# Sample tokens with the weights as the stationary operand: q, k, v of layer 1 of 2 and v, o of layer 2 of 2

## The chip, the core and the metric

The kernel runs on one NeuronCore of a Trainium2 chip. The metric is the device time of one execution in microseconds (us), the median of several runs. Five engines work side by side, each with its own queue: TensorE (PE in the profile; its weight loads have a row of their own, PEld), VectorE (DVE), ScalarE (ACT), GpSimd (POOL) and SyncE (SP), which here only issues DMAs.

A matmul on TensorE has two sides. `PE.matmul(out, l, r)` loads `l` into the array first (LDWEIGHTS, the stationary side) and then streams the columns of `r` through it (MATMUL, the moving side). The result has one partition per column of `l` and one column per column of `r`. The profile writes such a matmul as `128*16 128x512`: 128 rows by 16 stationary columns, then 128 rows by 512 moving columns.

## The reference

One inference step of a two-layer decoder trunk, for a prompt of 1024 tokens and eight sample tokens (one each of eight sequences with states of their own), 1032 tokens in all, model width 1024. Both layers normalise, project, mix and add the result to the residual:

```
u = hn @ w_in
# layer 0 (even): q | k | v | gate | z | xBC | dt
#   q, k: 8 heads of 64, partly rotated; dilated window attention, and a Mamba-2 scan
# layer 1 (odd):  q | k | v | o | i | f | z
#   mLSTM matrix memory, 8 heads of 256: h = sigmoid(o) * num / den, then head norm and silu(z)
```

The prompt goes through chunked forms of attention, scan and memory; each sample token takes one step against its cached keys and values or its state. All tensors are float32. What matters here are the products of the eight sample tokens' normalised activations with q, k, v (and dt) of layer 0, and with v and o of layer 1.

## The kernel before

Activations are kept transposed, feature on the partition: eight tiles `xh[k]` of 128 features by 1032 tokens. The matmuls take operands of type float32r. The kernel splits each float32 operand into a high part, its cast to float32r, and the remainder (`split`, L89: a ScalarE cast, then a subtraction on VectorE or GpSimd), `xh` and `xl` for activations, `wh`/`wl` and the like for weights, and `mm3` (L103) adds three products for each k: high by high, high by low, low by high.

**Layer 0, q, k, v (L517 to L574).** The loop runs over four groups `g` (two attention heads each, 128 columns each of q, k and v and four of dt: W1 = 388) and nine token blocks `b`. For b = 0 to 7 a block is 128 prompt tokens, for b = 8 the eight sample tokens. `qkv_block` takes the activations as the stationary side (128 or 8 columns) and 388 weight columns as the moving side: 24 matmuls into a PSUM tile `pq` from the pool of three banks (`MM`, L71). ScalarE copies q and k out, VectorE dt and v, GpSimd applies the rotation. For b = 8 the rows are stored at once to `qd`, `kd`, `vd` for the sample attention. The group's weights lie in four buffers of a ring of five (`w1p`, L308); `w1_fetch` splits the next group's as buffers come free. `qk_T` (L550) transposes q and k of the block before. `att_pump` (L511) takes steps of the prompt attention of earlier groups from a queue and puts them between; a `side` function runs in the middle of a block's matmuls.

The normalised activations come from `xn0_piece` (L324), in pieces of 256, 256 and 520 tokens; its `sink` (L223) scales and splits them. `sink` already knows a target `xs`, which nothing in layer 0 uses.

**Layer 1, v and o (L1464 to L1489).** For each of eight heads the weights `wv` are 1024 by 512 (256 columns of v, 256 of o). `vo_block` goes over nine blocks c. For c = 0 to 7 it is 24 matmuls of 128 stationary token columns by 512 weight columns. For c = 8 the stationary side is `xsm[:, k]`, 16 columns: the high parts of the eight sample tokens and then their low parts. Sixteen matmuls (8 k, high and low weights) give 16 rows of 512 in one PSUM tile, and ScalarE copies them out. Rows 0 to 7 and rows 8 to 15 go to the DRAM tile `svo` by four stores, and `dml_group` (L1367), which updates the samples' memory states for two heads at a time, loads both halves and adds them.

After each `vo_block(c)` comes `mstage(hd, c)` (L1491): `ml_prep(c)`, `ml_main(c - 1)` and `ml_out(c - 2)`, the chunked memory of the prompt. `ml_prep` makes the scores `mS`, `ml_main` the matmuls `mN` and `mC`, the state `Cst` and its split `mCh`, `mCl` for the next chunk, and the head norm `md`, `mx`; `ml_out` transposes `mx` into `mH`. Their PSUM tiles come from the pool of five banks (`X`, L74). So behind the sample block stand `ml_main(7)` and `ml_out(6)`, and the next head's projection `pf`.

A scheduler orders each engine's queue when the kernel is built: roughly the order of the program, but an instruction whose inputs it reckons ready can go ahead of one that would have to wait. The order is fixed before the kernel runs.

Of the kernel before, what the change touches and what calls it, by code (L numbers as in the profile page):

```python
# [7 lines left out]
F32R = mybir.dt.float32r  # L8
# [20 lines left out]
def body(ctx, tc, I, O):  # L29
# [35 lines left out]
    def SM(name, shape, bufs=2, dt=F32):  # L65
        return cur["sm"].tile(shape, dt, tag=name, name=name, bufs=bufs)
# [4 lines left out]
    def MM(name="mm"):  # L71
        return ps.tile([128, 512], F32, tag="mm", name=name, bufs=PS_MM)
# [10 lines left out]
    def C(name, shape, src=None, p=None):  # L83
        t = (p or cur["cst"]).tile(shape, F32, name=name)
        if src is not None:
            load(t, src)
        return t

    def split(hi, lo, src, eng=V):  # L89
        A.copy(hi, src)  # L90
        eng.tensor_tensor(lo, src, hi.bitcast(F32), sub)  # L91
# [80 lines left out]
    normw = C("normw", [128, 2, 8], I["normw"], gcst)  # L172
    ones = C("ones", [128, 128], None, gcst)
    G.memset(ones, 1.0)
    mhalf = C("mhalf", [128, 16], None, gcst)
    G.memset(mhalf, -0.5)

# [45 lines left out]
    def sink(src, wcol, pbs, hi, lo, eng=V, xs=None):  # L223
        scaled(src, src, wcol, pbs)
        split(hi, lo, src, eng)
        if xs is not None:
            split(xs[:, 0:8], xs[:, 8:16], src[:, 512:520])

    def pairs(tiles):
        return lambda k, c0, w: tiles[k // 2][:, (k % 2) * 520 + c0 : (k % 2) * 520 + c0 + w]  # L230
# [93 lines left out]
    def xn0_piece(i, c0, n):  # L324
        cs = slice(c0, c0 + n)
        box = {}

        def square(k):
            x = xs0[i](k)
            if i == 0:  # L330
                if k == 0:
                    t = S("acc")
                    box["acc"] = [t[:, :n], t[:, 512 : 512 + n]]
                hsum(box["acc"][k % 2], x, k < 2, k % 2 == 1)
                return
            if k == 0:
                box["acc"] = [TMP("acc")[:, :n]]
            hsum(box["acc"][0], x, k == 0)

        def stat():  # L340
            box["r"] = stat_r(box["acc"], n, 1.0 / 1024, 1.0)

        def bcast():
            box["p"] = r_bcast(box["r"], n)

        def out(k):
            sink(xs0[i](k), normw[:, 0, k : k + 1], box["p"], xh[k][:, cs], xl[k][:, cs], (V, G)[k % 2])

        return [lambda k=k: square(k) for k in range(8)], [stat, bcast], [lambda k=k: out(k) for k in range(8)]

# [160 lines left out]
    def att_pump(n, limit):  # L511
        for _ in range(n):
            if attq and attq[0][0] < limit:
                attq.popleft()[1]()


    def qkv_block(g, b, wp, side):  # L517
        m = 128 if b < 8 else 8
        c0 = b * 128
        p = MM("pq")  # L520
        terms = []
        for k in range(8):
            wv = slice((k % 2) * W1, (k % 2) * W1 + W1)
            terms.append((xh[k][:, c0 : c0 + m], xl[k][:, c0 : c0 + m], wp[k // 2][0][:, wv], wp[k // 2][1][:, wv]))
        mm3(p[:m, :W1], terms, side)
        qk = SM("qk", [128, 4, 64], 3)
        A.copy(qk[:m].rearrange("p a b -> p (a b)"), p[:m, 0:256])
        V.tensor_copy(dtr[:m, b, 4 * g : 4 * g + 4], p[:m, 384:388])
        ra = SM("ra", [128, 4, 16])
        cb = rot_c[:m, b : b + 1, :].broadcast_to([m, 4, 16])  # L530
        s1 = rot_s[:m, b : b + 1, 0:8].broadcast_to([m, 4, 8])
        s2 = rot_s[:m, b : b + 1, 8:16].broadcast_to([m, 4, 8])
        G.tensor_tensor(ra[:m, :, 0:8], qk[:m, :, 8:16], s1, mult)
        G.tensor_tensor(ra[:m, :, 8:16], qk[:m, :, 0:8], s2, mult)
        G.tensor_tensor(qk[:m, :, 0:16], qk[:m, :, 0:16], cb, mult)
        G.tensor_tensor(qk[:m, :, 0:16], qk[:m, :, 0:16], ra[:m], add)
        if b < 8:
            V.tensor_copy(vt[g][:, c0 : c0 + 128], p[:, 256:384])
            store(O["ak"][c0 : c0 + 128, g * 128 : g * 128 + 128], qk[:, 2:4, :].rearrange("p a b -> p (a b)"))
            return qk  # L540
        gs = slice(g * 128, g * 128 + 128)
        vs = SM("vs", [8, 128])
        A.copy(vs, p[:8, 256:384])
        store(O["aks"][:, gs], qk[:8, 2:4, :].rearrange("p a b -> p (a b)"))
        store(O["avs"][:, gs], vs)
        store(qd[:, gs], qk[:8, 0:2, :].rearrange("p a b -> p (a b)"))
        store(kd[:, gs], qk[:8, 2:4, :].rearrange("p a b -> p (a b)"))
        store(vd[:, gs], vs)

    def qk_T(g, b, qk):  # L550
# [4 lines left out]
        A.activation(qT[g][:, c0 : c0 + 128], pt[:, 0:128], AF.Copy, scale=-0.125)  # L555
        V.tensor_copy(kT[g][:, c0 : c0 + 128], pt[:, 128:256])

    for g in range(4):
        while len(w1r) < 4:
            w1r.append(w1_fetch(*w1q.popleft()))  # L560
        wp = [w1r.popleft() for _ in range(4)]
        qT[g], kT[g], vt[g] = S("qT"), S("kT"), S("vt")
        prev = None
        for b in range(9):
            qk = qkv_block(g, b, wp, [lambda: att_pump(2, g)] * 1)
            if prev is not None:
                qk_T(g, b - 1, prev)
            prev = qk
            if b == 7 and w1q:
                w1r.append(w1_fetch(*w1q.popleft()))  # L570
            att_pump(2, g)
            if g == 0 and b < 4:
                bpump((10, 16, 10, 0)[b])
        att_load(g)  # L574
    w1stack.close()
    wstack0 = ctx.enter_context(ExitStack())
    cur["w"] = pool("wp0", 2, wstack0)
# [467 lines left out]

        return f

    xsm = gcst.tile([128, 8, 16], F32R, name="xsm")
    hacc = st
    xh1, xl1 = [], []  # L1050

# [204 lines left out]

    hTd = D("hTd", [16, 128, NP])
    sqk = D("sqk", [2, 4, 8, 2, 256])
    svo = D("svo", [2, 2, 4, 8, 2, 256])
    mxs = C("mxs", [128, 4, 8])  # L1260
    mcv = C("mcv", [128, 32, 3])
    szs = C("szs", [128, 16, 8])
# [104 lines left out]
    def dml_group(g):  # L1367
        v32 = SM("v32", [16, 264], 1)
        o32 = SM("o32", [16, 256], 1)
        v2 = TMP("v2")[:16, :512].rearrange("p (j e) -> p j e", j=2)  # L1370
        for j, t in ((0, v32), (1, o32)):
            load(t[:, 0:256], svo[0, j, g].rearrange("b h e -> (b h) e"))
            load(v2[:, j], svo[1, j, g].rearrange("b h e -> (b h) e"))
        q = SM("dq", [128, 32], 1)
        kw = SM("dkw", [128, 32], 1)
        nn = dn4[:, g]
# [4 lines left out]
        num = SM("dnum", [128, 260], 1)  # L1381

        def prep():
            for j, t in ((0, v32), (1, o32)):
                V.tensor_tensor(t[:, 0:256], t[:, 0:256], v2[:, j], add)
            G.tensor_scalar(v32[:, 256:259], dg4[:, :, g], 1.0, None, mult)
            p = X("pvb")
            PE.matmul(p[:, 0:259], blkT, v32[:, 0:259], start=True, stop=True)
            A.copy(vb[:, 0:259], p[:, 0:259])
# [72 lines left out]
            wvr.append(wsplit(None, 1024, S("wvh", F32R), S("wvl", F32R), V, wvraw.popleft()))  # L1462

    def vo_block(hd, c, wv):  # L1464
        p = MM("pvo")
        g, h2 = divmod(hd["h"], 2)
        if c < 8:
            terms = []
            for k in range(8):
                o = (k % 2) * 512  # L1470
                terms.append((xh[k][:, c * 128 : c * 128 + 128], xl[k][:, c * 128 : c * 128 + 128], wv[k // 2][0][:, o : o + 512], wv[k // 2][1][:, o : o + 512]))
            mm3(p, terms)
            vv = (R("mvh", [128, VC]), R("mvl", [128, VC]))
            for u in range(2):
                G.tensor_scalar(vv[u][:, 256:VC], two[:, u], 1.0, None, mult)
            split(vv[0][:, 0:256], vv[1][:, 0:256], p[:, 0:256])
            tho = SM("mtho", [128, 256])
            A.activation(tho, p[:, 256:512], AF.Tanh, scale=0.5)
            hd["v", c] = (vv, tho)
        else:  # L1480
            for k in range(8):
                o = (k % 2) * 512
                for u in range(2):
                    PE.matmul(p[:16], xsm[:, k], wv[k // 2][u][:, o : o + 512], start=k == 0 and u == 0, stop=k == 7 and u == 1)
            vo8 = TMP("vo8")[:, :512]
            A.copy(vo8[:16], p[:16])
            for u in range(2):
                for j in range(2):
                    store(svo[u, j, g, :, h2], vo8[u * 8 : u * 8 + 8, j * 256 : j * 256 + 256])  # L1489

    def mstage(hd, c):  # L1491
        if c < 8:
# [22 lines left out]
    for h in range(8):  # L1515
# [51 lines left out]
        wv = [wvr.popleft() for _ in range(4)]  # L1567
        hd["C"] = SM("Cst", [128, 2, VC], 1)
        for c in range(9):
            vo_block(hd, c, wv)  # L1570
            if c == 1:
                p = X("pms")
                PE.transpose(p[:32, 0:128], t.rearrange("p a b -> p (a b)"), ident)
                t2 = TMP("mst2")[:32, :128]
                V.tensor_copy(t2, p[:32, 0:128])
                for j in range(4):
                    store(sqk[j // 2, g, :, h2, (j % 2) * 128 : (j % 2) * 128 + 128], t2[j * 8 : j * 8 + 8])
            mstage(hd, c)
            if c == 2 and h2:
                pump(1)  # L1580
            if c == 7 and h:
                dml_load(*((g, 0) if h2 else (g - 1, 3)))
# [281 lines left out]
```

## Time and profile before

| what | us |
| --- | --- |
| median of 3 runs | 2126.53 |
| lowest and highest | 2125.18, 2133.5 |
| the profiled execution | 2130.37 |
| its span, first instruction to last | 2128.5 |

Mean granted clock of TensorE in the profiled execution: 0.997 of full speed.

The profile is of one execution. Its page gives for each engine the busy time, and a chain followed back from the last instruction. A row of a group reads: line, engine, operation, output<-inputs, shapes, xcount | busy us, mean ns of one | idle time before them and who ended it. A row of the timeline reads: start us, duration us, engine, line, operation, output<-inputs, shapes, count. Durations of matmuls overlap, because they are pipelined; what one costs in a row of many is the distance from start to start. A row of the windows view reads: stretch, its length, then busy time and count for PE, PEld, DVE, ACT and POOL, then the granted clock of TensorE, the DMA engines' share and GB/s.

### The profile page before, as it was taken

To read this page: it belongs to the slowest core of one execution; us is meant where nothing else is said; L and a number is where in the kernel's file an instruction comes from. 1 tells how busy PE (TensorE), PEld (TensorE's weight loads), DVE (VectorE), ACT (ScalarE), POOL (GpSimd) and SP (SyncE) were. 2 spreads that over 40 slices of the span, in tenths; PEclk is the share of its full clock that TensorE was granted. 3 is DMA by queue.
4 is the path that set the end of the run, shared out by engine and by line. 5 is a ranking of instruction groups with operands and counts; after the bars stand their busy time and mean duration, and the time that the engine had idled before them with its cause. 6 is when DMAs were issued, how large, how long until landed. Compare 5 with 4: busy or idle time off the path is not lost.

```text
span 2128.5 us, 35218 instructions
## 1 busy us (share of the span) xinstructions
PE 2088.0 (98%) x12926; PEld 1873.7 (88%) x12926; DVE 1348.8 (63%) x3208; ACT 869.3 (41%) x1901; POOL 478.0 (22%) x1004
## 2 busy tenths in 40 slices
PE   7999999999999999999999999999999999999998
PEld 6877778998898899989899898898998988987798
DVE  7444478879987657546457565584665755756744
ACT  5434344456644334424335343253342533434321
POOL 4222100114310001241321522314214133141000
PEclk9999999999999999999999999999999999999999
DMA  5222053226575543312114133141331322416742
GB/s 162 73 74 79 14 163 105 85 75 194 185 226 167 169 162 60 90 35 85 50 64 135 41 111 98 40 145 44 99 117 37 116 78 78 140 31 213 268 163 96
DMA packets 162077, 232.30 MB, mean 109 GB/s; under 512 B 41200, under 2 KB 106976, under 8 KB 161904
## 3 DMA queue, kind: packets, MB, share of 16 engines
q1 hardware_dynamic: 161904, 230.04, 34.5%
q8 instruction: 102, 1.67, 0.3%
q14 instruction: 71, 0.58, 0.1%
HBM read 174.35 MB, written 55.62 MB: 108 GB/s over the span
## 4 chain that ended last, share of the span: by engine, by line
PE 85%; DVE 4%; DMA 2%; POOL 2%; ACT 2%; issue 1%; SPq 0%; POOLq 0%; DVEq 0%; ACTq 0%
PE pf L112 36%; PE pvo L112 16%; PE po L931 14%; PE pq L112 4%; PE mN L112 2%; PE mC L112 2%; PE pS L428 2%; PE pO L487 1%; PE mS L1294 1%; PE pT L470 1%; PE py L771 1%; POOL mCl L91 1%; PE mH L1355 1%; PE psl L777 1%; PE mS L1296 1%
## 5 line engine op out<-in xcount | busy, mean ns | idle before, releaser
L112 PE MATMUL pf<-yh,wh 128*128 128x344 f32 x1152 | 370.2, 321 | 0.0
L112 PE MATMUL pf<-yl,wh 128*128 128x344 f32 x1152 | 368.9, 320 | 0.0
L112 PE MATMUL pf<-yh,wl 128*128 128x344 f32 x1152 | 368.5, 320 | 0.0
L91 DVE TENSOR_TENSOR wl<-raw,wh 128x1024 fp32r<-128x1024 f32 x128 | 159.0, 1242 | 146.1 <-ACT wh L90 145.3
L90 ACT CAST wh<-raw 128x1024 fp32r<-128x1024 f32 x128 | 134.2, 1049 | 256.9 <-PE po L931 99.6
L112 PEld LDWEIGHTS pf<-yh,wh 128*128 128x128 f32 x1152 | 216.9, 188 | 1.3 <-ACT craw L242 1.0
L112 PEld LDWEIGHTS pf<-yl,wh 128*128 128x128 f32 x1152 | 216.5, 188 | 0.0
L112 PEld LDWEIGHTS pf<-yh,wl 128*128 128x128 f32 x1152 | 216.4, 188 | 0.0
L112 PE MATMUL pvo<-wvh,yh 128*128 128x512 f32 x512 | 206.3, 403 | 0.0
L112 PE MATMUL pvo<-wvh,yl 128*128 128x512 f32 x512 | 202.0, 394 | 0.0
L112 PE MATMUL pvo<-wvl,yh 128*128 128x512 f32 x512 | 201.5, 394 | 0.0
L112 PE MATMUL pf<-xh,wh 128*128 128x344 f32 x576 | 191.6, 333 | 0.0
L112 PE MATMUL pf<-xl,wh 128*128 128x344 f32 x576 | 186.8, 324 | 0.0
L112 PE MATMUL pf<-xh,wl 128*128 128x344 f32 x576 | 186.7, 324 | 0.0
L1282 DVE TENSOR_SCALAR mx<-mx,mbs,md 128x256 f32<-128x256 f32 x64 | 26.4, 413 | 177.7 <-POOL md L1281 177.7
L250 DVE SCALAR_TENSOR_TENSOR cout<-craw,mcw,cout 128x1024 f32<-128x1024 f32 x96 | 123.3, 1285 | 14.0 <-ACT cout L248 11.9
L931 PE MATMUL po<-oh,wl 128*128 128x512 f32 (+2 forms) x384 | 123.4, 322 | 2.8 <-DVE wl L91 2.7
L931 PE MATMUL po<-oh,wh 128*128 128x512 f32 (+2 forms) x384 | 123.6, 323 | 1.2 <-ACT oh L90 1.2
L931 PE MATMUL po<-ol,wh 128*128 128x512 f32 (+2 forms) x384 | 123.7, 323 | 0.0
L112 PEld LDWEIGHTS pvo<-wvh,yl 128*128 128x128 f32 x512 | 96.2, 188 | 22.6
L112 PEld LDWEIGHTS pvo<-wvh,yh 128*128 128x128 f32 x512 | 96.3, 188 | 20.6 <-issue 1.3
L112 PEld LDWEIGHTS pvo<-wvl,yh 128*128 128x128 f32 x512 | 96.3, 188 | 20.0
(440 smaller groups left out, 4995.7 us busy)
## 6 DMA issues: line engine op xcount, KB each, us to landing
raw<-in_wo SPq DMA_DIRECT2D x56, 512.0 KB
raw<-in_wq SPq DMA_DIRECT2D x32, 512.0 KB
raw<-in_wvo SPq DMA_DIRECT2D x32, 512.0 KB
dC<-in_mcs SPq DMA_DIRECT2D x32, 512.0 KB
out_mcs<-dC SPq DMA_DIRECT2D x32, 512.0 KB
raw<-in_wf SPq DMA_DIRECT2D x24, 512.0 KB
sE<-acd SPq DMA_DIRECT2D x16, 512.0 KB
raw<-in_wz SPq DMA_DIRECT2D x16, 512.0 KB
```

The lines of the kernel that those rows point to most:

```text
L90: A.copy(hi, src)
L91: eng.tensor_tensor(lo, src, hi.bitcast(F32), sub)
L112: PE.matmul(out, l, r, start=i == 0, stop=i == n - 1)
L250: V.scalar_tensor_tensor(o[:, :NP], raw[:, j : j + NP], w4[:, j : j + 1], o[:, :NP], mult, add)
L428: PE.matmul(p[:, :n], qT[g][hs, qs], kT[g][hs, ks], start=True, stop=True)
L470: PE.transpose(pt[:, h * n + k : h * n + k + 128], P[:, k : k + 128], ident)
L487: PE.matmul(po[h * 64 : h * 64 + 64, qs], v, PT[:, h * n + k * 128 : h * n + k * 128 + 128], start=j + k == 0, stop=j == 7 and k == nk - 1)
L771: PE.matmul(o, xd[:, h], Ev[:, h], start=True, stop=True)
L777: PE.matmul(pl, bt, xx[:, 512:1024], start=True, stop=True)
L931: PE.matmul(p[:, :m], wt[:, ws], at, start=i == 0 and q == 0, stop=i == nk - 1 and q == 2)
L1282: V.tensor_scalar(x, x, bs[:, 6:7], d[:, 2:3], sub, mult)
L1294: PE.matmul(pS[:, 0:128], hd["k"][j][:, tok], hd["q"][j][:, tok], start=j == 0, stop=j == 1)
```

## The change

Both sample projections swap their sides. A new helper `sample_cols` takes 128 weight columns at a time as the stationary side and the 16 columns `xsm[:, k]` as the moving side: for each column block m, 16 matmuls (8 k, high and low weights) into 16 columns of one PSUM tile from the pool of five. ScalarE copies the tile out, and VectorE adds the columns of the high parts to those of the low parts, which leaves the result with the weight column on the partition and the eight samples along the row. `sample_rows` turns it back: one transpose of 8 columns per block m. For layer 1 there are four blocks of 128; for layer 0 there are three of 128 and one of 4 (dt).

`xsm` is now filled in layer 0 too, in the last piece of `xn0_piece`. In layer 0 the block b = 8 returns a function that does the transposes and the rest of the old work; it runs in the middle of the next group's first block, or after the loop for the last group. In layer 0 this uses four products (high and low of both) in place of three. In layer 1 the transposes, the copy and two stores in place of four run after `mstage(hd, 8)`; `svo` loses its leading dimension, and `dml_group` two loads and two additions.

```diff
+    xsm = gcst.tile([128, 8, 16], F32R, name="xsm")
...
+    def sample_cols(n, w):
+        p = X("pxs")
+        nm = -(-n // 128)
+        ends = [min(128, n - 128 * m) for m in range(nm)]
+        for m, e in enumerate(ends):
+            for k in range(8):
+                for u in range(2):
+                    PE.matmul(p[:e, 16 * m : 16 * m + 16], w(k, u)[:, 128 * m : 128 * m + e], xsm[:, k], start=k == 0 and u == 0, stop=k == 7 and u == 1)
+        parts = TMP("parts")
+        pv = parts[:, : 16 * nm].rearrange("p (m u t) -> p m u t", m=nm, u=2)
+        sv = parts[:, 64 : 64 + 8 * nm].rearrange("p (m t) -> p m t", m=nm)
+        full = n // 128
+        for m0, m1, e in ((0, full, 128), (full, nm, ends[-1])):
+            if m1 > m0:
+                A.copy(parts[:e, 16 * m0 : 16 * m1], p[:e, 16 * m0 : 16 * m1])
+                V.tensor_tensor(sv[:e, m0:m1], pv[:e, m0:m1, 0], pv[:e, m0:m1, 1], add)
+        return sv, ends
+
+    def sample_rows(sv, ends):
+        p = X("pxr")
+        for m, e in enumerate(ends):
+            PE.transpose(p[:8, 128 * m : 128 * m + e], sv[:e, m], ident[:e, :e])
+        return p
...
-            sink(xs0[i](k), normw[:, 0, k : k + 1], box["p"], xh[k][:, cs], xl[k][:, cs], (V, G)[k % 2])
+            sink(xs0[i](k), normw[:, 0, k : k + 1], box["p"], xh[k][:, cs], xl[k][:, cs], (V, G)[k % 2], xsm[:, k] if c0 + n == T else None)
...
+        if b == 8:
+            sv = sample_cols(W1, lambda k, u: wp[k // 2][u][:, (k % 2) * W1 : (k % 2) * W1 + W1])
+            att_pump(2, g)
+            return lambda: qkv_out(g, b, sample_rows(*sv))
...
-            qk = qkv_block(g, b, wp, [lambda: att_pump(2, g)] * 1)
+            qk = qkv_block(g, b, wp, [lambda: (att_pump(2, g), late.popleft()() if late else None)] * 1)
...
+            if b == 8:
+                late.append(qk)
...
+    late.popleft()()
...
-            load(t[:, 0:256], svo[0, j, g].rearrange("b h e -> (b h) e"))
-            load(v2[:, j], svo[1, j, g].rearrange("b h e -> (b h) e"))
+            load(t[:, 0:256], svo[j, g].rearrange("b h e -> (b h) e"))
...
-            for k in range(8):
-                o = (k % 2) * 512
-                for u in range(2):
-                    PE.matmul(p[:16], xsm[:, k], wv[k // 2][u][:, o : o + 512], start=k == 0 and u == 0, stop=k == 7 and u == 1)
-            vo8 = TMP("vo8")[:, :512]
-            A.copy(vo8[:16], p[:16])
-            for u in range(2):
+            sv = sample_cols(512, lambda k, u: wv[k // 2][u][:, (k % 2) * 512 : (k % 2) * 512 + 512])
+
+            def finish():
+                vo8 = TMP("vo8")[:8, :512]
+                A.copy(vo8, sample_rows(*sv)[:8])
                 for j in range(2):
-                    store(svo[u, j, g, :, h2], vo8[u * 8 : u * 8 + 8, j * 256 : j * 256 + 256])
+                    store(svo[j, g, :, h2], vo8[:, j * 256 : j * 256 + 256])
+
+            return finish
...
-            vo_block(hd, c, wv)
+            fin8 = vo_block(hd, c, wv)
...
             mstage(hd, c)
+            if fin8:
+                fin8()
```

More of the change, by code (lines that the diff above doesn't have):

```diff
@@ L525, in qkv_block, with qkv_out @@
         mm3(p[:m, :W1], terms, side)
+        return qkv_out(g, b, p)
+    def qkv_out(g, b, p):
+        m = 128 if b < 8 else 8
+        c0 = b * 128
         qk = SM("qk", [128, 4, 64], 3)
@@ L556, in qk_T @@
         V.tensor_copy(kT[g][:, c0 : c0 + 128], pt[:, 128:256])
+    late = deque()
     for g in range(4):
@@ L1046, in operand @@
         return f
-    xsm = gcst.tile([128, 8, 16], F32R, name="xsm")
     hacc = st
@@ L1258, in body @@
     sqk = D("sqk", [2, 4, 8, 2, 256])
-    svo = D("svo", [2, 2, 4, 8, 2, 256])
+    svo = D("svo", [2, 4, 8, 2, 256])
     mxs = C("mxs", [128, 4, 8])
@@ L1369, in dml_group @@
         o32 = SM("o32", [16, 256], 1)
-        v2 = TMP("v2")[:16, :512].rearrange("p (j e) -> p j e", j=2)
         for j, t in ((0, v32), (1, o32)):
-            load(t[:, 0:256], svo[0, j, g].rearrange("b h e -> (b h) e"))
-            load(v2[:, j], svo[1, j, g].rearrange("b h e -> (b h) e"))
+            load(t[:, 0:256], svo[j, g].rearrange("b h e -> (b h) e"))
         q = SM("dq", [128, 32], 1)
@@ L1383, in prep @@
         def prep():
-            for j, t in ((0, v32), (1, o32)):
-                V.tensor_tensor(t[:, 0:256], t[:, 0:256], v2[:, j], add)
             G.tensor_scalar(v32[:, 256:259], dg4[:, :, g], 1.0, None, mult)
@@ L1464, in vo_block @@
     def vo_block(hd, c, wv):
-        p = MM("pvo")
         g, h2 = divmod(hd["h"], 2)
         if c < 8:
+            p = MM("pvo")
             terms = []
```

## The prediction

> **What bounds the kernel now.** I read the page first: the busy shares and the chain that ended last.
>
> ```profile
> span 2128.5 us, 35218 instructions
> PE 2088.0 (98%) x12926; PEld 1873.7 (88%) x12926; DVE 1348.8 (63%) x3208; ACT 869.3 (41%) x1901; POOL 478.0 (22%) x1004
> PE 85%; DVE 4%; DMA 2%; POOL 2%; ACT 2%; issue 1%; SPq 0%; POOLq 0%; DVEq 0%; ACTq 0%
> PE pf L112 36%; PE pvo L112 16%; PE po L931 14%; PE pq L112 4%; PE mN L112 2%; PE mC L112 2%; PE pS L428 2%; PE pO L487 1%; PE mS L1294 1%; PE pT L470 1%; PE py L771 1%; POOL mCl L91 1%; PE mH L1355 1%; PE psl L777 1%; PE mS L1296 1%
> ```
>
> TensorE is busy 98% and carries 85% of the chain, so a microsecond added to its stream is a microsecond of the end. Only its waits can give something back. What matters is the start-to-start spacing of its instructions, which the timeline gives (time, duration, engine, line):
>
> ```profile
> 942.26 0.40 PE L1484 MATMUL pvo<-wvl,xsm 128*16 128x512 f32 x1
> ...
> 945.53 0.39 PE L1484 MATMUL pvo<-wvl,xsm 128*16 128x512 f32 x1
> 66.29 0.34 PE L112 MATMUL pq<-w1h,xh 128*8 128x388 f32 x1
> ...
> 67.17 0.34 PE L112 MATMUL pq<-w1h,xl 128*8 128x388 f32 x1
> ```
>
> The first pair is the 2nd and the 16th sample matmul of a head: 3.27 us in 14 steps, **0.234 us** each. The second pair is five steps of a layer-0 sample block: **0.176 us** each. Both are set by the moving columns (512, 388), the short stationary load beside them hidden.
>
> **The change part by part.** The stationary side becomes 128 weight columns and the moving side 16, so the weight load is what remains. The groups of loads by form, and the two places where loads meet almost no moving columns:
>
> ```profile
> L112 PEld LDWEIGHTS pvo<-wvl,yh 128*128 128x128 f32 x512 | 96.3, 188 | 20.0
> L1296 PEld LDWEIGHTS mS<-ident,cout 128*128 128x128 f32 x128 | 16.2, 142 | 0.0
> L1484 PEld LDWEIGHTS pvo<-wvl,xsm 128*16 128x16 f32 x64 | 6.1, 95 | 7.8
> L188 PEld LDWEIGHTS pst<-ones,yacc 128*128 128x128 f32 x16 | 2.2, 191 | 0.0
> 2032.65 0.98 PEld L188 LDWEIGHTS pst<-ones,yacc 128*128 128x128 f32 x8
> L858 PE MATMUL psy<-ident,so 8*128 8x8 f32 x8 | 0.7, 204 | 0.0
> 629.29 0.66 PE L858 MATMUL psy<-ident,so 8*128 8x8 f32 x8
> ```
>
> Eight pairs of a 128-column load and a one-column matmul (pst) take 0.98 us from the first load's start to the last one's end; without that last load's 0.191 us, seven steps of **0.113 us**. The transposes psy take (0.66 - 0.204)/7 = **0.065 us**. Which one prices the new pairs? This kernel's own fp32r loads last 188 ns at 128 columns and 95 at 16, 0.83 ns a column, as the pst loads do (191); transposing loads take 142. So I take 0.113 and keep 0.065 as the low end. From above, load and matmul laid end to end bound it at about 0.12, since the 16 columns cost 16/512 of 0.234.
>
> *Layer 1, each of 8 heads.* Removed: 16 x 0.234 = 3.74 us. Added: four blocks of 16 pairs, 64 x 0.113 = 7.23 us. Added after the stage: four transposes of an 8-column stationary against the identity. Their spacing comes from two transposes with the same 128 moving columns:
>
> ```profile
> 67.35 0.38 PE L554 MATMUL pqk<-ident,qk 128*128 128x128 f32 x2
> L554 PE MATMUL pqk<-ident,qk 128*128 128x128 f32 x64 | 12.0, 274 | 0.7 <-POOL qk L536 0.7
> ```
>
> (0.38 - 0.27) = 0.11, so 0.44 us. Net +3.93 a head, **+31.4 us**.
>
> *Layer 0, each of 4 groups.* Removed: 24 x 0.176 = 4.22 us. Added: three full blocks, 48 x 0.113 = 5.42, and one of four columns, 16 pairs at 0.065 (between 0.02 and 0.113) = 1.04, and 0.39 of transposes. Net +2.63, **+10.5 us**.
>
> *Off TensorE.* The new PSUM copies, adds and the final copy lie beside other TensorE work. fin8 runs after the matmuls of mstage(hd, 8), the layer-0 transposes in the middle of the next group's first block, so those matmuls cover copy and add; uncovered they would cost about 0.5 us each time (a small cast and a subtraction take 0.19 and 0.35 in the xsm rows below). For the last group no block follows, but queued attention does. The svo stores go from four to two a head and two loads and two adds a group disappear. SP's queue gets shorter, and nothing on the path waits for it: **0**.
>
> *What is given back.* TensorE's waits, from the view of waits (total, times, longest):
>
> ```profile
> PE mH L1355 <- DVE mx L1282: 4.5, 8, 1.0
> PE mN L112 <- POOL mCl L91: 1.2, 3, 0.4
> ```
>
> The eight mH waits are one a head, right behind the sample block. A block 3.5 us longer lets the mx chain finish: **-5** (0 to -5.7).
>
> *Start.* Layer 0 now fills xsm too, eight casts and eight subtractions; the rows are those of the same work in layer 1:
>
> ```profile
> L90 ACT CAST xsm<-h x8: 193/194/197, 807.3 to 812.8; 128x8 fp32r<-128x8 f32 x8
> L91 DVE TENSOR_TENSOR xsm<-h,xsm x8: 153/352/701, 808.0 to 813.2; 128x8 fp32r<-128x8 f32 x8
> ```
>
> VectorE is the slower side of that loop: 8 x 0.15 to 0.35 = 1.2 to 2.8 us, part of it behind block b=4's matmuls: **+1** (0 to 3).
>
> *Weights of the next group.* The five-buffer ring frees a w1 buffer when its last reader ends. The old order (k outside) freed one every six matmuls; the new one (column block outside) frees all in the last, short block. The casts and subtractions queued behind:
>
> ```profile
> 65.30 1.88 POOL L91 TENSOR_TENSOR w1l<-raw,w1h 128x776 fp32r<-128x776 f32 x1 [0.35 <-ACT w1h L90]
> ...
> 66.49 0.84 ACT L90 CAST w1h<-raw 128x776 fp32r<-128x776 f32 x1 [0.20 <-PE pq L112]
> ```
>
> One buffer is ready after 0.84 + 1.88 = 2.7 us. The tail block and the next group's first two k steps (1.0 + 12 x 0.176/2) cover some 2.1: about 0.7 at each of three changes, **+2** (0 to 6). The sample block also moves from the pool of three PSUM banks to the pool of five that mS, mN, mC and mH use; its first matmul may wait for the mkl that reads the oldest: **+2** (0 to 3).
>
> Sum: 31.4 + 10.5 - 5 + 1 + 2 + 2 = **+42 us** as long as the clock holds. The profiled execution took 2130.4 (span 2128.5), the median is 2126.5; the difference moves both alike, so 2168.5.
>
> **The clock.** The windows view has the granted clock (PEclk, after the busy times):
>
> ```profile
> 338.96:342.37 3.41, 3.41 (x11) 1.66 (x9) 1.70 (x6) 0.80 (x3) 0.00 (x0) 1.00 0.02 5
> 342.37:345.78 3.41, 3.41 (x15) 2.85 (x14) 1.34 (x6) 0.00 (x0) 0.00 (x0) 0.50 0.00 0
> 1994.42:1997.83 3.41, 1.15 (x5) 0.98 (x6) 3.41 (x7) 0.17 (x1) 0.00 (x0) 1.00 0.98 321
> 1997.83:2001.25 3.42, 3.42 (x10) 2.64 (x9) 3.42 (x9) 0.46 (x1) 0.00 (x0) 0.50 0.99 361
> ```
>
> Twice the clock fell to 0.50 for one window of 3.41 us, each time after a window with few matmuls. The later one held five of 512 columns (2,560 columns), behind an idle stretch. The earlier one reads busy (by modelled ends), but held few columns:
>
> ```profile
> L428 PE MATMUL pS<-kT,qT 64*128 64x256 f32 x4 | 2.5, 724 | 0.0
> L112 PE MATMUL pf<-xh,wl 128*128 128x344 f32 x2 | 0.7, 373 | 0.0
> L112 PE MATMUL pf<-xh,wh 128*128 128x344 f32 x2 | 0.7, 346 | 0.0
> L470 PE MATMUL pT<-ident,P 128*128 128x128 f32 x2 | 0.6, 300 | 0.0
> L112 PE MATMUL pf<-xl,wh 128*128 128x344 f32 x1 | 0.3, 321 | 0.0
> ```
>
> 4 x 256 + 5 x 344 + 2 x 128 = 3,000 columns. The new blocks stream 30 pairs x 16 = **480 columns** in such a window, for 6.4 us (layer 0) or 7.2 us (layer 1). If the gate counts what streams, each block holds a whole poor window and the clock falls in all twelve; if it counts loads too, it holds. No row separates these; the column count fits both falls, so I give falling more.
>
> The Trainium skill ("TensorE: Matmul & The Clock Gate", Part 1) ties the half clock to an idle window of about 3.4 us. By that rule a block without idle time keeps its clock, which is rival A below; the trace speaks against it at 338.96, where TensorE reads busy throughout and the clock still fell, though modelled ends may hide short gaps there.
>
> Price of a fall, from rows at half clock: the first pst of the kernel, whose matmuls last 353 ns where later ones last 234, and po in the second fall's window:
>
> ```profile
> 8.47 2.14 PE L188 MATMUL pst<-ones,acc 128*128 128x1 f32 x8 [8.47 <-DVE acc L217]
> L188 PE MATMUL pst<-ones,acc 128*128 128x1 f32 x8 | 2.0, 353 | 8.6 <-DVE acc L217 8.5
> L188 PE MATMUL pst<-ones,yacc 128*128 128x1 f32 x16 | 2.2, 234 | 0.0
> 1999.72 0.63 PE L931 MATMUL po<-oh,wl 128*128 128x512 f32 x1
> ...
> 2000.57 0.63 PE L931 MATMUL po<-ol,wh 128*128 128x512 f32 x1
> ```
>
> A pair then takes (2.14 - 0.353)/7 = 0.255, a 512-column matmul 0.425. The fall comes at the end of the first whole window, 3.4 to 6.8 us into a block, 5.1 on average. In layer 1 the 2.1 us left become 4.7 (+2.6), and about 5 us of dense work behind it runs at half pace until a window has filled again, losing 45%, 2.3: **+5 a head** (3.4 to 7.3), 40 us. In layer 0 1.3 us are left, +1.6 and 2.3: **+4 a group**, 16 us. Together 42 + 56 = **+98 us, 2224.5**.
>
> **The rivals.**
> *A, the clock holds:* 2168.5. For it: loads keep the array occupied all through. Against it: 338.96.
> *B, the clock falls in each block:* 2224.5. For it: both falls.
> *C, A with a queue block.* ScalarE's copy of the new PSUM tile, and VectorE's add behind it, wait for the whole sample block. If they are queued ahead of the state's update, that chain starts only then:
>
> ```profile
> 942.01 0.87 DVE L1337 SCALAR_TENSOR_TENSOR Cst<-Cst,scl,mC 128x258 f32<-128x258 f32 x2
> ...
> 944.17 0.61 ACT L90 CAST mCh<-Cst 128x516 fp32r<-128x516 f32 x1
> ...
> 944.87 1.32 POOL L91 TENSOR_TENSOR mCl<-Cst,mCh 128x516 fp32r<-128x516 f32 x1 [1.04 <-ACT mCh L90]
> ```
>
> 2.8 us less the first mN matmuls, 2.4 a head, and about 4 in layer 0: +23 on A, 2191.5. Against it: Cst starts at 942.01 beside the block's first matmuls, with everything it needs, so a copy that waits for the block's end has no reason to stand ahead of it.
> *D, not slower:* the load is cheap, at the psy price. 704 pairs x (0.113 - 0.065) = 34 us less than A: 2134.5. Each 0.01 us of a pair is 7 us; below 0.068 the change is within 0.5%. Against it: fp32r loads of 188 ns, not 142.
>
> **How the numbers follow.** B 0.50, A 0.34, C 0.10, D 0.06. Forecast: 2224.5. B's own range is 2200 to 2240. The range goes from A's low end (short pairs at 0.02, a full give-back, no stalls: 2157) to B's upper end, 2240; it leaves out D and the tails. About 0.5% (10.6 us) can be told from no change: A, B and C are slower, 0.94; D is the same, 0.05, or with a little more, faster, 0.01.
>
> **What would show it.** Right: new pairs 0.113 apart before any fall; PEclk at 0.50 for whole 3.41 us windows after each sample block and a mean clock near 0.97 to 0.98 against 0.997; mH waits gone. A shows the same spacing and a clock of 1.00. C shows TensorE waiting for mCl or mCh once a head. D shows pairs under 0.07. Wrong altogether: TensorE's stream no longer the bound, or blocks broken up by other matmuls so that no window is poor.

## The result, and the profile after

| | before | after |
| --- | --- | --- |
| median, us | 2128.79 (5 runs) | 2214.05 (5 runs) |
| lowest and highest | 2125.18, 2133.5 | 2213.57, 2216.5 |
| ratio, 95% interval | | 1.0407 (1.0395 to 1.0419) |
| the profiled execution | 2130.37 | 2216.5 |
| its mean granted clock | 0.997 | 0.969 |

The change makes the kernel 4.1% slower, 85 us. The page of the changed kernel, the lines that answer to those of before:

```profile
span 2214.7 us, 36427 instructions
PE 2180.0 (98%) x13518; PEld 1987.2 (90%) x13518; DVE 1358.7 (61%) x3224; ACT 869.7 (39%) x1925; POOL 478.9 (22%) x1004
PE 84%; DVE 2%; ACT 1%; DMA 1%; POOL 1%; issue 1%; SPq 0%; POOLq 0%; DVEq 0%; ACTq 0%
PE pf L112 36%; PE pvo L112 16%; PE po L969 13%; PE pxs L237 4%; PE mN L112 3%; PE mC L112 2%; PE mS L1331 1%; PE pq L112 1%; PE pS L453 1%; PE pO L512 1%; PE pT L495 1%; PE py L809 1%; PE mH L1392 1%; PE mS L1333 1%; PE psl L815 0%
```

TensorE is busy 98% as before, in a span that is 86 us longer. The new pairs (pxs) hold 4% of the chain, some 89 us by that rounded share, though 704 pairs at 0.112 us would be 79 and the matmuls they replace took 47. So their price alone is not the whole loss.

The timeline shows that price (start, duration, engine, line), with the clock at 1.00 up to 68.97 us and at 0.50 behind it:

```profile
64.13 0.26 PE L237 MATMUL pxs<-xsm,w1h 128*128 128x16 f32 x1
64.24 0.26 PE L237 MATMUL pxs<-xsm,w1l 128*128 128x16 f32 x1
...
68.93 0.33 PE L237 MATMUL pxs<-xsm,w1l 128*128 128x16 f32 x1
69.11 0.36 PE L237 MATMUL pxs<-xsm,w1h 128*128 128x16 f32 x1
...
69.75 0.36 PE L237 MATMUL pxs<-xsm,w1l 128*128 128x16 f32 x1
69.97 0.17 PE L237 MATMUL pxs<-xsm,w1h 128*4 128x16 f32 x1
...
70.36 0.17 PE L237 MATMUL pxs<-xsm,w1l 128*4 128x16 f32 x1
```

From 64.13 to 68.93 are 43 steps: **0.112 us** a pair. From 69.11 to 69.75 are three steps at half clock: 0.214. The short block's 15 steps from 69.97 to 70.36, still at half clock, take 0.026 each.

The windows view around the sample block of the first head of layer 1, which begins at 964.1 (after the busy times of PE, PEld, DVE, ACT and POOL stands the granted clock):

```profile
963.26:966.67 3.41, 3.41 (x32) 3.31 (x30) 2.81 (x12) 0.91 (x2) 0.71 (x3) 1.00 0.08 19
966.67:970.08 3.41, 3.41 (x19) 3.41 (x18) 0.41 (x1) 0.00 (x0) 2.27 (x4) 0.50 0.14 38
970.08:973.50 3.42, 3.42 (x18) 3.42 (x18) 0.00 (x0) 0.00 (x0) 0.00 (x0) 0.50 0.02 5
973.50:976.91 3.41, 3.41 (x17) 3.41 (x18) 0.19 (x1) 0.21 (x1) 0.00 (x0) 0.50 0.00 0
976.91:980.33 3.42, 3.42 (x18) 3.09 (x18) 2.24 (x10) 0.05 (x1) 0.43 (x2) 0.50 0.11 38
980.33:983.74 3.41, 3.41 (x23) 3.41 (x23) 0.98 (x5) 0.52 (x1) 0.98 (x3) 1.00 0.27 82
```

The clock falls inside the block, for four whole windows, and comes back only after a window of dense work (mN, mC, the transposes). TensorE and its loads read busy all the time; what is missing is moving columns (whether that is the cause, e3 and e5 test). The same happens in each of the twelve blocks: in layer 0 stretches of 6.83, 6.83, 10.24 and 6.83 us at half clock (30.7 together), in layer 1 between 6.83 and 13.65 us a head (88.7 together). Before, two windows of 3.41 us fell, apart from the end.

The view of waits answers to that of before (total us, times, longest):

```profile
PE pO L512 <- DVE PT L500: 2.1, 5, 0.6
PE pxs L237 <- DVE mkl L1340: 1.4, 2, 0.8
...
PE pq L112 <- DVE w1l L91: 0.2, 1, 0.2
```

The 4.5 us of mH waits and the 1.2 us of mN waits are gone; the new block waits twice for its PSUM tile.

Where the 86 us lie can be read from the first pvo matmul of layer 1's first and last head. Before, then after:

```profile
878.71 0.51 PE L112 MATMUL pvo<-wvh,yh 128*128 128x512 f32 x1
...
1852.80 0.50 PE L112 MATMUL pvo<-wvh,yh 128*128 128x512 f32 x1
```

```profile
900.70 0.51 PE L112 MATMUL pvo<-wvh,yh 128*128 128x512 f32 x1
...
1930.50 0.50 PE L112 MATMUL pvo<-wvh,yh 128*128 128x512 f32 x1
```

| stretch, us | before | after | more |
| --- | --- | --- | --- |
| start to the first pvo (layer 0 among it) | 878.7 | 900.7 | 22.0 |
| one head, mean of seven | 139.16 | 147.11 | 7.95 |
| last head's pvo to the end | 275.7 | 284.2 | 8.5 |

22.0 + 7 x 7.95 + 8.5 = 86.2, the difference of the spans.

### The profile page after: what moved, and what is told of

It is laid out like the page before. It is cut to its first block, busy times and chain, and to the rows that moved or that the text cites. A ratio compares the mean times of both kernels' runs of the same rounds, so it can differ in the third digit from the quotient of the medians.

```text
span 2214.7 us, 36427 instructions
## 1 busy us (share of the span) xinstructions
PE 2180.0 (98%) x13518; PEld 1987.2 (90%) x13518; DVE 1358.7 (61%) x3224; ACT 869.7 (39%) x1925; POOL 478.9 (22%) x1004
## 4 chain that ended last, share of the span: by engine, by line
PE 84%; DVE 2%; ACT 1%; DMA 1%; POOL 1%; issue 1%; SPq 0%; POOLq 0%; DVEq 0%; ACTq 0%
PE pf L112 36%; PE pvo L112 16%; PE po L969 13%; PE pxs L237 4%; PE mN L112 3%; PE mC L112 2%; PE mS L1331 1%; PE pq L112 1%; PE pS L453 1%; PE pO L512 1%; PE pT L495 1%; PE py L809 1%; PE mH L1392 1%; PE mS L1333 1%; PE psl L815 0%
```

## The experiments

The theory: a pair of a 128-column load and 16 moving columns costs 0.112 us, more than what it replaces; and since so little streams, the clock falls in each block. The rivals: the clock answers to the loads and not to the columns; the clock costs little and the loads carry it all; the new waits do.

**One layer at a time.** e1 keeps the new form in layer 0 alone, e2 in layer 1 alone; the other layer's functions are those of before.

> Only layer 0 in the new form; layer 1 as in the kernel before. Theory (loads at 0.111 us a pair, and a clock that falls because few columns stream): per group 48 x 0.111 + 16 x 0.03 + 0.4 - 4.2 = +2.0 and about +3.7 for a fall (30.7 us at half clock over four groups, half of it lost), with +1 for the start: +24, about 2153 us (2146 to 2158); half clock behind each of the four blocks, none in layer 1 but the old one near 1998. Rival (the clock costs next to nothing, the loads carry it all): +60 or so of the 85 would have to sit in layer 1, and this run gives 2140 or less.

> Only layer 1 in the new form; layer 0 as in the kernel before. Theory: per head 64 x 0.111 + 0.4 - 3.74 = +3.8, less 0.56 of mH wait, plus 5.5 for a fall (88.7 us at half clock over eight heads, half of it lost): +8.7 a head, about 2198 us (2188 to 2203). With e1 the two parts add up to the whole change within 3 us. Rival (the parts share a cost, as a common wait): the two gains over the kernel before don't add up to 85.

e1: 2153.1 us (2148.39 to 2159.54) against 2129.31, ratio 1.0116 (1.0095 to 1.0137). e2: 2188.54, ratio 1.0281 (1.0265 to 1.0296). Both lie in their ranges, e2 at the low end. 23.8 + 59.2 = 83.0 of 85: the parts add up, and layer 1 carries most. The runs of e1 lie 11 us apart, those of the whole change 3. In e1's profile the half-clock stretches of the four groups are 6.83, 3.41, 10.24 and 6.83 us, one window fewer than in the change; the number can differ between executions. The mean clocks of e1's four runs go with their times: 0.991, 0.988, 0.988 and 0.986 for 2148.39, 2152.82, 2153.38 and 2159.54 us. Only the first has a trace, so where the others lost their clock isn't shown.

**The same loads with more columns.** e3 lets each sample matmul stream its 16 columns eight times over (`reps` is (8,)):

```diff
+                r = reps[k % len(reps)]
+                xr = xsm[:, k].unsqueeze(1).broadcast_to([128, r, 16])
                 for u in range(2):
-                    PE.matmul(p[:e, 16 * m : 16 * m + 16], w(k, u)[:, 128 * m : 128 * m + e], xsm[:, k], start=k == 0 and u == 0, stop=k == 7 and u == 1)
+                    PE.matmul(p[:e, 128 * m : 128 * m + 16 * r].rearrange("p (r t) -> p r t", r=r), w(k, u)[:, 128 * m : 128 * m + e], xr, start=k == 0 and u == 0, stop=k == 7 and u == 1)
...
```

The copy behind it, not shown here, then reads the first 16 of each 128 columns.

> Same loads, same order; each sample matmul streams 128 columns (its 16 repeated eight times) where the change streams 16, some 30 x 128 = 3,840 a window. Theory (the gate counts what streams): pair spacing stays at 0.111 us since the load sets it, the clock holds in all twelve blocks, 2155 to 2172 us at a mean clock of 0.995 or more. Rival 1 (the gate answers to the loads, or to their share of the window): falls as in the change, 2210 to 2225. Rival 2 (the clock follows something else in the new blocks, as the wait for PSUM): the same as rival 1.

2184.39 us (2178.8 to 2186.39), ratio 1.0264 (1.0247 to 1.0281): 30 us faster than the change, but slower than the 2155 to 2172 expected. In the profiled execution the mechanism is as the theory has it: the spacing stays 0.112 us (the load hides 128 columns as it hides 16), and the clock holds in all twelve blocks (two falls are left inside the run, at 214.5 and 1969.0, each behind a stall of TensorE). Two steps of e3:

```profile
69.52 0.28 PE L239 MATMUL pxs<-xsm,w1l 128*128 128x128 f32 x1
...
69.74 0.28 PE L239 MATMUL pxs<-xsm,w1l 128*128 128x128 f32 x1
```

Two windows inside a block of the same form (in e6, below), where the granted clock stays at 1.00:

```profile
964.40:967.80 3.40, 3.40 (x33) 3.40 (x32) 1.76 (x10) 0.92 (x2) 1.30 (x2) 1.00 0.17 46
967.80:971.20 3.40, 3.40 (x33) 3.40 (x32) 0.41 (x1) 0.00 (x0) 1.29 (x4) 1.00 0.02 5
```

Loads are as many and as dense as in the change, so they don't pull the clock. That execution is the fastest of the four, 2178.8 us at a mean clock of 0.995; the other three, 2184 to 2186 us, have 0.989 or 0.990, so they spent more time at half clock, and no trace shows where. What kept the time up is another thing, and it stands in the view of waits and the timeline of ScalarE in the last head:

```profile
PE pxr L253 <- DVE parts L247: 8.8, 1, 8.8
```

```profile
1973.35 1.04 ACT L90 CAST oh<-hld 128x1024 fp32r<-128x1024 f32 x1 [1.61 <-DMA hld<-hTd]
1974.30 0.20 ACT L246 COPY parts<-pxs 128x64 f32<-128x64 f32 x1
1976.87 0.57 ACT L1520 COPY vo<-pxr 8x512 f32<-8x512 f32 x1 [2.36 <-PE pxr L253]
```

The pairs of that block ended at 1964.7, but the copy of the tile stands in ScalarE's queue behind casts that wait for DMAs, and the transposes behind the copy. The queue's order is fixed when the kernel is built; why the scheduler put the copy there (it may reckon these matmuls slower than they are) isn't shown. TensorE stands idle, and the clock falls for 10.24 us. This is rival C of the prediction at another place: the change itself doesn't have it, its copy stands in front of those casts.

**Spread over the stage.** e4 leaves layer 0 as in the change. In layer 1 it computes the four column blocks at four places, with 16 columns (`sample_part`, not shown here, is `sample_cols` for a single block):

```diff
+            if c in (1, 3, 5):
+                if c == 1:
+                    svt[0] = SM("svt", [128, 4, 8], 1)
+                sample_part(svt[0], 512, c // 2, lambda k, u: wv[k // 2][u][:, (k % 2) * 512 : (k % 2) * 512 + 512])
         else:
-            sv = sample_cols(512, lambda k, u: wv[k // 2][u][:, (k % 2) * 512 : (k % 2) * 512 + 512])
+            sv = sample_part(svt[0], 512, 3, lambda k, u: wv[k // 2][u][:, (k % 2) * 512 : (k % 2) * 512 + 512])
```

> Layer 0 as in the change; in layer 1 the same 64 pairs of 16 columns a head, but a quarter each behind the vo blocks 1, 3, 5 and at the old place, so that no window is without dense matmuls (16 pairs are 1.8 us; the other 1.6 us stream some 3,500 columns). Theory: the clock holds in layer 1, 88.7 / 2 = 44 us come back, less up to 8 x 1 us of mH waits that are covered less: 2170 to 2182 us, half-clock windows left in layer 0 alone. Rival (loads as such pull the clock or the time): nothing comes back, 2205 to 2220.

2201.14 us, ratio 1.034 (1.0324 to 1.0355): 13 us back, where 32 to 44 were expected. The clock did come back: in layer 1 three windows fall instead of 26. But the view of waits shows what was given up:

```profile
PE mN L112 <- POOL mCl L91: 7.4, 7, 1.5
PE mH L1403 <- DVE mx L1330: 5.4, 7, 0.8
```

The sample block stands between the state's update and its next reader. In the change it is 7 us long and hides both chains; here 1.8 us of it are left at that place, less than the 3.7 of before, and 12.8 us of waits appear (before: 5.7). I had counted mH alone. A head takes 144.8 us ((1919.21 - 905.47) / 7), 2.3 less than in the change and 2.7 more than with the clock held and no such waits (142.08, e6 below). Of these 2.7, the waits are some 1.8 and the two falls in these seven heads, by estimate, 0.5; the rest stays unexplained. Layer 0, though built from the same lines, came 4.8 us later than in the change (905.47 against 900.70), with 37.6 us at half clock instead of 30.7.

**Where the clock trips.** e5 takes e3's form with another width for each block; 104, 100 and 88 are means of two widths over k. In layer 1 the call becomes (layer 0 likewise, with 128, 112, 96 and 64 for its four groups):

```diff
-            sv = sample_cols(512, lambda k, u: wv[k // 2][u][:, (k % 2) * 512 : (k % 2) * 512 + 512])
+            sv = sample_cols(512, lambda k, u: wv[k // 2][u][:, (k % 2) * 512 : (k % 2) * 512 + 512], ((8,), (7,), (7, 6), (7, 6, 6, 6), (6,), (6, 5), (5,), (3,))[hd["h"]])
```

> One look, for the place of the threshold. Same loads; the columns of a sample matmul differ from block to block: in layer 0 128, 112, 96, 64 for the four groups, in layer 1 128, 112, 104, 100, 96, 88, 80, 48 for the eight heads (104 and 100 as means over k). At 30.7 pairs a window that is 3930, 3440, 3195, 3070, 2950, 2700, 2460, 1475 columns. Theory (the gate counts columns and trips between the 3,000 and the 3,228 of the kernel before): the clock holds for 128, 112 and perhaps 104, falls for 96 and all below, in both layers. Rival (the gate counts time in which matmuls are in flight, or loads): no edge between 96 and 112; all heads alike.

One execution was taken, at 2195.95 us (the kernel before: 2128.86); what counts is its trace.

| head of layer 1 | columns a matmul | columns a window (30.5 pairs) | the clock in the block |
| --- | --- | --- | --- |
| 0 | 128 | 3900 | holds |
| 1 | 112 | 3420 | holds |
| 2 | 104 | 3170 | holds |
| 3 | 100 | 3050 | falls |
| 4 to 7 | 96, 88, 80, 48 | 2930 to 1460 | falls |

The windows view of heads 2 and 3:

```profile
1250.18:1253.59 3.41, 3.41 (x33) 3.41 (x32) 1.52 (x7) 1.18 (x3) 2.76 (x5) 1.00 0.14 41
1253.59:1257.00 3.41, 3.41 (x32) 3.41 (x31) 2.87 (x8) 0.21 (x1) 0.00 (x0) 1.00 0.22 89
...
1393.58:1397.00 3.42, 3.42 (x33) 3.42 (x33) 0.41 (x1) 0.04 (x1) 2.29 (x4) 1.00 0.14 38
1397.00:1400.40 3.40, 3.40 (x18) 3.40 (x18) 0.19 (x1) 0.21 (x1) 0.00 (x0) 0.50 0.00 0
```

The first and the third row are the windows to compare. In each, 33 matmuls and their loads (32 or 33) keep TensorE busy from end to end. What differs is the moving columns: 3,216 start in the first, 3,008 in the other, and only the other is followed by half clock. A matmul more or less at a window's end is 96 to 112 columns. Layer 0 agrees in part: its groups with 128 and 112 hold and the one with 64 falls. The group with 96 doesn't count, because the window that its block fills (205.77 to 209.18) keeps its clock, with the short pairs in it, and the fall at 212.59 comes behind a stall of TensorE (3.79 us, for PT). So in these blocks the gate answers to what streams, and for these float32r matmuls the edge is between about 3,010 and 3,220 columns in 3.41 us. The rival by loads or by matmuls in flight is out.

The edge is not one for all matmuls. In e6 the window from 40.91 to 44.33 has 14 matmuls with some 1,500 columns, ten of them plain float32 and four transposes, and an idle stretch of 0.9 us, and the clock holds behind it. Why isn't shown. The prediction cited a rule of the Trainium skill ("TensorE: Matmul & The Clock Gate", Part 1), by which an idle window halves the clock. By the time for which TensorE has instructions no window of the sample blocks is idle and the rule would let the clock hold; it agrees with the trace only if a window with few columns counts as idle, loads or not.

**e3 without its stall, and layer 0 by itself.** e6 is e3 with 16 columns in the last head, which puts the copy back ahead of the casts. e7 also turns layer 0's loops (k outside, one PSUM bank a column block), so that weight buffers come free during the block. e8 is e7 with 16 columns in layer 0.

```diff
-            sv = sample_cols(512, lambda k, u: wv[k // 2][u][:, (k % 2) * 512 : (k % 2) * 512 + 512])
+            sv = sample_cols(512, lambda k, u: wv[k // 2][u][:, (k % 2) * 512 : (k % 2) * 512 + 512], (8,) if hd["h"] < 7 else (1,))
```

and for e7 and e8 besides, with `banks` true in layer 0:

```diff
-        p = X("pxs")
+        ps_ = [X("pxs") for m in range(nm)] if banks else [X("pxs")] * nm
...
-        for m, e in enumerate(ends):
-            for k in range(8):
+        order = [(k, m) for k in range(8) for m in range(nm)] if banks else [(k, m) for m in range(nm) for k in range(8)]
+        for k, m in order:
```

> As e3 (128 moving columns), but head 7 with 16, so that ScalarE's copy of its block stands ahead of the oh casts again; e3 lost 8.8 us there to a copy queued behind casts that wait for DMA, and a fall after it. Theory: heads 0 to 6 at the 142.1 us of e3, head 7 with one fall, the end as in the change: 2168 to 2176 us. Rival (the 142.1 us hides a cost that shows elsewhere): 2180 or more.

> As e6, but layer 0's sample block runs k outside and column blocks inside (one PSUM bank for each column block), so that a w1 buffer is released every quarter of the block, as in the kernel before. Theory (half of layer 0's loss is the next group's casts and subtractions, which all start at the block's end and push TensorE's PT and pq operands back): the first pvo comes at 888 to 893 us where e3 has 897.8 and the kernel before 878.7; 6 to 10 us less than e6. Rival (layer 0's loss is the pairs and transposes): within 2 us of e6.

> As e7 with layer 0's sample matmuls at 16 columns: layer 0's clock falls again. Theory (falls cost layer 0 little in the change because the waits for weights lie in the same time; without these waits the falls show): 8 to 15 us more than e7. Rival (a fall costs layer 0 nothing in itself): within 3 us of e7.

e6: 2177.67 us, ratio 1.0236 (1.0222 to 1.025), a little above the 2168 to 2176 expected. Its first and last pvo:

```profile
900.79 0.51 PE L112 MATMUL pvo<-wvh,yh 128*128 128x512 f32 x1
...
1895.38 0.50 PE L112 MATMUL pvo<-wvh,yh 128*128 128x512 f32 x1
```

A head takes (1895.38 - 900.79) / 7 = 142.08 us: 2.92 more than before, 5.03 less than in the change. That is the price of loads and transposes, and the price of the falls. (e3, e7 and e8 give 142.14, 141.99 and 142.03; e2, with the falls, 146.59.) But layer 0 ends as late as in the change (900.8, 900.7), though its clock holds in the four blocks and e6 has only 10.2 us at half clock up to there, in three windows elsewhere (the change 34.1). Other executions say much the same: with the clock held in these blocks the first pvo comes at 897.8 in e3, where the falls are left at 901.0 in e1 and 905.5 in e4. So the falls are worth some 3 us in layer 0, no more than one form differs between executions. Something else fills most of their place, and the waits of e6 show a part of it:

```profile
PE pO L514 <- DVE PT L502: 5.4, 5, 3.6
PE pxr L253 <- DVE kT L592: 1.6, 2, 0.8
PE pq L112 <- POOL w1l L91: 1.2, 2, 0.6
```

The longest of them in the timeline of VectorE (this one is from e3, whose layer 0 is the same):

```profile
210.88 1.95 DVE L91 TENSOR_TENSOR w1l<-raw,w1h 128x776 fp32r<-128x776 f32 x1 [6.96 <-DMA vc<-vcd]
212.75 1.86 DVE L247 TENSOR_TENSOR parts<-parts 128x24 f32<-128x24 f32 x2
214.54 0.40 DVE L502 COPY PT<-pT 128x256 f32<-128x256 f32 x1
```

VectorE's subtraction for the next group's weights and the adds of the sample block stand ahead of the copy PT for which the attention waits. In the change the same waits are 0.2 us (w1l) and 2.1 (PT); that TensorE reaches these operands later at half clock is the reading that fits, and no run shows it alone.

e7: 2177.35 us, the same as e6; first pvo at 900.9, where 888 to 893 was expected. By the time alone the rival came true. The waits for w1l are gone and those for PT fell from 5.4 to 2.2, as the theory has it, but four banks of the pool of five are now held for a whole block, and a new wait of the same size stands in the gain's place:

```profile
PE pS L458 <- ACT parts L246: 5.3, 2, 3.0
```

e8: 2180.92 us, ratio 1.0242 (1.0225 to 1.0259), first pvo at 905.4. Its median is 3.6 us above e7's, but the runs overlap (2174.39 to 2182.06 against 2174.53 to 2180.19), so the two can't be told apart. Expected were 8 to 15 us; that the falls cost layer 0 little in itself, the rival, is nearer. (e7 isn't free of falls either: two follow its new wait, 10.2 us at half clock.) What the rest of layer 0's loss is beyond pairs and transposes, and how much of it a better order of the queues would bring back, stays open.

**A version that beats both.** e9 goes the other way: the old sides, but one stationary side of 40 columns in both layers, hi in 0 to 7 and lo in 32 to 39 (the columns between belong to other k, and their rows aren't read). Layer 0 then needs 16 matmuls a group in place of 24, and the halves are added off TensorE:

```diff
+    def sample(p, n, w):
+        for k in range(8):
+            for u in range(2):
+                PE.matmul(p[:40, :n], xsmf[:, 8 * sx(k) : 8 * sx(k) + 40], w(k, u), start=k == 0 and u == 0, stop=k == 7 and u == 1)
+        lo = TMP("slo")
+        A.copy(lo[:8, :n], p[32:40, :n])
+        V.tensor_tensor(lo[:8, :n], lo[:8, :n], p[:8, :n], add)
+        return lo
```

> A version that should beat both: the orientation of before (activations stationary, weights moving), but in both layers with one 40-column stationary side, hi in columns 0 to 7 and lo in 32 to 39, so that layer 0 needs 16 matmuls a group where it had 24, and the sum of both halves is a copy and an add off TensorE. 4 x 8 x 0.176 = 5.6 us less in layer 0, nothing changed in layer 1's stream: 2121 to 2126 us, a ratio of 0.997 to 0.999. Rival (the copy and the add stand in front of something on the path): 2129 or more.

2126.4 us against 2127.51, ratio 0.9992 (0.9983 to 1.0001): no difference that can be told, and just outside the 2121 to 2126 expected. Layer 0 gained what was worked out (first pvo 873.0 against 878.7), layer 1 gave most of it back: its mH waits rose from 4.5 to 7.0 us and its mN waits from 1.2 to 2.0. So e10 keeps it in layer 0 alone.

> The 40-column stationary side in layer 0 alone, layer 1 word for word as in the kernel before. In e9 layer 0 came 5.7 us earlier (first pvo 873.0 against 878.7) and layer 1 gave most of it back (mH waits 7.0 against 4.5 us, mN 2.0 against 1.2), behind its longer copy and add. Theory: the 5.7 us stay, 2121 to 2124 us, a ratio of 0.997 to 0.998. Rival (the order of the later stages shifts with any edit and gives as much back): 2126 or more.

2122.66 us against 2130.5, ratio **0.9965** (0.9951 to 0.9978), where 0.997 to 0.998 was expected. It is the fastest form of all. Its first pvo starts at 872.4, 6.3 us earlier than before, and layer 1's waits stay as they were:

```profile
PE mH L1380 <- DVE mx L1307: 4.6, 8, 1.0
PE mN L112 <- POOL mCl L91: 1.4, 4, 0.5
```

In its profile the span is 9.4 us shorter than in that of before, 3 us more than layer 0 explains. They lie behind the last pvo, where the fall at 1997.83 and a part of the wait ahead of it are missing (po waits 1.0 us for wl, before 2.7). e1, whose layer 1 is that of before, has no such fall there either and ends 271.8 us after its last head's first pvo (e10 272.3, before 275.7), so these 3 us need not belong to the edit.

## Why the prediction was right, and where its sizes were off

The forecast was 2224.5 us, the measured median 2214.05. The mechanism held, and layer 1's part of the sum came out nearly whole; layer 0's falls were the term that was much too big. The loads cost more than the matmuls they replace, and the clock falls in all twelve blocks for whole windows of 3.41 us (mean clock 0.969; 0.97 to 0.98 was given).

- **Pairs at 0.113 us:** 0.112 measured. The low end of 0.065, on which the rival "not slower" stood, was far off.
- **Short pairs at 0.065 us:** 0.026, even at half clock; a load of four columns costs hardly anything. The term was 0.6 us a group too high.
- **Layer 1 while the clock holds, +3.93 less 0.56 of mH waits a head:** 3.4, and e6 shows 2.92. The mH waits are gone, as said; so are the mN waits.
- **Falls in layer 1, +5 a head:** 5.03, but from two errors that cancel. A half-clock pair takes 0.214 us and not 0.255 (I took that from pst, whose two sides are plain float32 and at whose time, 8.47 us, the trace has no record of the clock: the first begins at 18.10), while the slow stretch lasts 11.1 us a head (88.7 / 8) and not the 9.7 (4.7 + 5) of the sum. 11.1 x (1 - 0.112 / 0.214) = 5.3.
- **Layer 0:** 10.5 of pairs and transposes, 16 of falls, 1 for the start and 2 for the next group's weights were 29.5; 22.0 was measured up to the first pvo. The start is right (the first sample block begins at 64.13, before at 63.05). The term that failed is the 16 for the falls. I had laid it on top of everything else, but where the clock holds in the blocks (e3, e6) layer 0 ends only some 3 us earlier than where it falls, and waits appear instead. In e6 those for PT, kT and w1l are 8.2 us, before 1.7. The 2 us for weights were thus too small as a price with the clock up, and next to nothing with it down (0.2 for w1l). With the short pairs at 0.026, pairs and transposes are 8 and not 10.5; of e6's 22.1 us, these 8, the start and the 6.5 of added waits make 15.5, and what the rest is stays open.
- **PSUM pool, +2:** 1.4 us in two waits.
- **Rival A (the clock holds), 2168.5:** e6, whose last head still falls, took 2177.7; less some 5 for that head it is about 2173, an estimate, since e6 also has three half-clock windows in layer 0. The term for the falls, 56, is then 41 in the whole kernel.
- **The columns of the falls before:** the 3,000 that I counted in the window at 338.96 take in matmuls that began before it; 1,968 columns start there, in part in pS, which is plain float32. By the same count the 3,228 named in e5's expectation (the window at 24.93, which held) is 2,452. That these two figures enclose the edge that e5 found was luck. They could fix no edge, and that few columns make the clock fall rests on e3 and e5.
- **The low end of the range:** its named terms (short pairs at 0.02, a give-back of 5.7, no stalls) give 2161, not 2157; nothing hangs on it.
- **Rival C (the copy in a queue):** absent from the change, but it appeared in e3, at the place where other work waits for DMA, and cost 8.8 us and a fall.

## What to carry to other kernels

Swapping the sides pays only if the loads that are added cost less than the columns that are saved: here a 128-column float32r load costs 0.112 us and 512 moving columns 0.234, so for eight tokens four loads (0.45 us) cost nearly twice what they replace. Count the moving columns of a block in windows of 3.41 us: here a block of 7 us with too few of them ran at half clock and took the dense work behind it along, 5.03 us a head. The edge has to be measured for the matmuls at hand. And before a block that stands in front of a dependence is moved or shortened, look up what it hides: in e4 the waits it uncovered, 12.8 us, ate a good part of the gain.

## What the runs showed of the hardware

- Loads don't keep the clock up: with TensorE and PEld busy from end to end the clock fell after a window in which 3,008 float32r columns started and held after one with 3,216 (e5).
- Up to 128 moving columns are free behind a 128-column load: the spacing is 0.112 us with 16 (the change) and with 128 (e3). They can serve to hold the clock; in layer 1 that is worth 5.03 us a block (147.11 against e6's 142.08).
- At half clock the load-bound spacing nearly doubles too (0.112 to 0.214), so here the loads slow with the granted clock.
